# Five of eleven gate/up blocks of both SwiGLU sub-layers as seven products of halves, with the modulation sums at other blocks

## The chip, the cores and the metric

One core of a Trainium2 chip runs the whole layer in one launch. The metric is the device time of that core in microseconds, the median of three runs. Products run on TensorE (PE; its weight loads are PEld), elementwise work on VectorE (DVE), ScalarE (ACT) and GpSimd (POOL); SyncE (SP) issues the loads.

## What is computed

A decoder layer for 512 tokens of width 1024, all in float32. Only the two SwiGLU sub-layers and the conditioning bear on the change:

```python
def swiglu(h, w_gu, w_dn):
    g, u = jnp.split(h @ w_gu, 2, axis=-1)          # w_gu: 1024 x 5632, w_dn: 2816 x 1024
    return (jax.nn.silu(g) * u) @ w_dn

mods = (jax.nn.silu(c) @ w_ada[l] + b_ada[l]).reshape(B, N_MOD, 1, D_MODEL)
sh1, sc1, gt1, sh2, sc2, gt2, sh3, sc3, gt3 = [mods[:, i] for i in range(N_MOD)]
h = rmsnorm(x, g_pre[l, 0]) * (1 + sc1) + sh1
x = x + 0.5 * gt1 * rmsnorm(swiglu(h, w_gu1[l], w_dn1[l]), g_post[l, 0])
...
h = rmsnorm(x, g_pre[l, 2]) * (1 + sc3) + sh3
x = x + 0.5 * gt3 * rmsnorm(swiglu(h, w_gu2[l], w_dn2[l]), g_post[l, 2])
```

Between them stands the token mixer (gated linear attention beside softmax attention), which the change does not touch.

## The kernel before

**Products in three parts.** Every float32 operand is held as a pair of TensorE's float32r tiles, a rounded high part and the low part that is left (`hilo`, L197; for weights `split`, L152: ScalarE casts the raw tile to the high part at L155, VectorE subtracts at L156). A product is three matmuls, high by high, high by low and low by high (`PARTS`, L188).

**A gate/up block** (`ffn`, L381) makes 256 columns of gate and the same 256 of up, for 512 tokens; there are 11 blocks (jb = 0 to 10) in each of the two sub-layers. A block loads four raw weight tiles of 128 x 4 x 256 (512 KB each: `gw` and `uw`, first and second half of the 1024 input features), splits each, and issues 4 x 8 x 3 = 96 matmuls of 512 columns (`gu_matmuls`, L371) into four accumulators. Block 0 of the second sub-layer issues 192 of 256 columns instead, since its two halves of tokens come ready one after the other. The end of a block is tanh on ScalarE (L399), two fused operations on VectorE (L400, L401) and a high and a low part of the result (L403), twice.

**What sets the order.** A tile framework gives each tile a buffer from a ring by its tag and each engine a queue that it works through in order. The rings that matter: 4 raw tiles (`raw`, L148), 5 high and 5 low weight tiles (`whi`, `wlo`), 4 temporaries (`t2`), 69 units of 128 x 512, 6 accumulators (`mm`). A tile waits until the last reader of the tile that had its buffer is done. SyncE's queue holds the loads in the order of the program.

**The modulation sums** (`mod_cols`, L251) are columns of the conditioning for the next sub-layer: 8 loads of 256 KB into 4 raw tiles and 8 operations on VectorE (`ada_acc`, L202), then 4 tiny matmuls and 3 tiny operations. Four of them, handed over as `extra`, are taken in blocks 1, 3, 5 and 7 of the first sub-layer (L390). The second sub-layer has none.

`make_h` (L342) and `modulated` (L472) make the normalised input h of the second and the first sub-layer in temporaries and keep only its high and low parts.

Of the kernel before, what the change touches and what calls it, by code (L numbers as in the profile page):

```python
# [39 lines left out]
def tile_hybrid_layer(  # L40
# [24 lines left out]
    def tmp(shape=(P, 512), dt=F32):  # L65
        return sb.tile(list(shape), dt, tag="t2", bufs=NTMP, name=nm("t2"))
# [4 lines left out]
    def acc(shape=(P, 512)):  # L71
        return pm.tile(list(shape), F32, tag="mm", name=nm("mm"))
# [206 lines left out]
    def mod_gate(g, i, h, factor):  # L279

        c0 = (3 * i + 2) * D + h * 512
        gs = unit()
        g.append(gs)
        tc.keep_in_program_order(nc.sync.dma_start(gs, g_post[i, h * 512:(h + 1) * 512].partition_broadcast(P)))
        br = tmp()
        nc.sync.dma_start(br[0:1], b_ada[c0:c0 + 512].unsqueeze(0))

        def src(raw, kh):
            nc.sync.dma_start(raw, w_ada[kh * 256:(kh + 1) * 256, c0:c0 + 512].rearrange("(k p) c -> p k c", p=P))
        a = ada_acc(src)  # L290
        nc.vector.tensor_tensor(a[0:1, :], a[0:1, :], br[0:1], ALU.add)
        ps = aux()
        hi, lo = two_parts(a)
        nc.tensor.matmul(ps, ones_r, hi, start=True, stop=False)
        nc.tensor.matmul(ps, ones_r, lo, start=False, stop=True)
        nc.vector.scalar_tensor_tensor(gs, ps, factor, gs, ALU.mult, ALU.mult)
# [42 lines left out]
                nc.tensor.transpose(ps[:, j, e * P:(e + 1) * P], xn[e][d // 4][:, (d % 4) * P:(d % 4 + 1) * P], ident)  # L339
        return ps  # L340

    def make_h(tp, hs, shc, scc):  # L342

        xn = [x_norm(2 * tp + e, x_stat(2 * tp + e)) for e in range(2)]
        ts = slice(tp * 256, (tp + 1) * 256)
        for dp in range(4):
            ps = x_turned(tp, xn, dp)
            ht = tmp((P, 2, 256))
            for j in range(2):
                d = 2 * dp + j  # L350
                nc.vector.tensor_scalar(ht[:, j], ps[:, j], scc[:, d:d + 1], shc[:, d:d + 1], ALU.mult, ALU.add)
                hilo(hs[d][0][:, ts], hs[d][1][:, ts], ht[:, j], nc.gpsimd)
# [91 lines left out]
    with in_order(last):  # L444
        ada = []
        for ch in range(4):
            ada.append(ada_fetch_first(ch))
            if ch % 2 == 0:
                for b in first:
                    b.fetch(2 * ch, 2 * ch + 4)  # L450
        rs_ = []
        xn = []

        def norm(t):

            xx = sb.tile([P, D], F32, tag="wlo", bufs=NW, name=nm("xn"))
            for h in range(2):
                nc.vector.tensor_scalar(xx[:, h * 512:(h + 1) * 512], xt[t][h], rs_[t], None, ALU.mult)
            xn.append([xx[:, 0:512], xx[:, 512:1024]])

        for t in range(NT):
            rs_.append(x_stat(t))
            if t == 1:
                norm(0)
                small_columns()

        def turn(tp, dp, eng):
            ps = x_turned(tp, xn[2 * tp:2 * tp + 2], dp, (aux, acc)[dp % 2])
            for j in range(2):
                eng(xT[2 * dp + j][:, tp * 256:(tp + 1) * 256], ps[:, j])  # L470

        def modulated(ch, a, n):  # L472

            mod_turn(sh1, sc1, 0, ch, mod_reduce(a))
            ht = [tmp() for _ in range(2)]
            for e in range(2):
                d = 2 * ch + e
                nc.vector.tensor_scalar(ht[e], xT[d], sc1[:, d:d + 1], sh1[:, d:d + 1], ALU.mult, ALU.add)
            if ch < 3:
                ada_sum_a(ada[ch + 1], range(n))  # L480
            for e in range(2):
                d = 2 * ch + e
                hilo(hs[d][0], hs[d][1], ht[e])
            if ch < 3:
                ada_sum_a(ada[ch + 1], range(n, ROWS_A[ch + 1]))

        norm(1)
        norm(2)
        for dp in range(4):
            turn(0, dp, nc.vector.tensor_copy)  # L490
            if dp == 0:
# [649 lines left out]
```

## Time and profile before

| | us |
|---|---|
| median of 3 runs | 1454.02 (1453.26 to 1456.02) |
| profiled execution, its own time | 1452.96 |
| its span, first to last instruction | 1451.2 |
| TensorE busy | 1399.9 |
| VectorE busy | 765.7 |
| ScalarE busy | 531.4 |

The last three rows are busy time within the span. What lies around the span is 1452.96 - 1451.2 = 1.8 us. Matmuls are pipelined, so a duration of one matmul in the profile is longer than its share of the engine; start-to-start distances tell the rate. Durations on VectorE and ScalarE are those of one instruction; two that follow each other overlap by about 0.1 us.

### The profile page before, as it was taken

The numbers are of one execution on the slowest core, as the hardware profiler recorded it, in microseconds if no ns is written. First come the engines' busy times: TensorE is split into PE (matmuls) and PEld (weight loads), VectorE is DVE, ScalarE is ACT, GpSimd is POOL, SyncE is SP. The second block draws the span as 40 slices with busy tenths as digits, with TensorE's granted clock in tenths as the row PEclk, the third lists the DMA queues.
The fourth block names the chain that finished last, engine by engine and source line by source line (L and its number), as shares of the span: only waits on it lengthen the run. The fifth ranks groups of instructions, "written<-read, shape, count | busy, mean of one in ns | idle before, by whom it ended". The sixth has DMA issues, their size and how long they took to land.

```text
span 1451.2 us, 17081 instructions
## 1 busy us (share of the span) xinstructions
PE 1399.9 (96%) x6477; PEld 1124.3 (77%) x6477; DVE 765.7 (53%) x1210; ACT 531.4 (37%) x915; POOL 203.8 (14%) x328
## 2 busy tenths in 40 slices
PE   4899999999999999999999999999999999999998
PEld 3688888878877777767888887788888888887886
DVE  6945544372266689762745546538464334337232
ACT  5332322232244376653723333423353322222221
POOL 6200000000041643340110202100060000000001
PEclk7999999999999999999999999999999999999999
DMA  9444543272235846212232232125613223325411
GB/s 323 156 147 145 156 148 102 59 246 99 90 120 163 241 135 182 82 40 91 87 106 84 59 87 59 59 73 163 204 55 116 87 91 100 100 87 184 136 58 58
DMA packets 156463, 173.36 MB, mean 119 GB/s; under 512 B 8778, under 2 KB 123574, under 8 KB 156380
## 3 DMA queue, kind: packets, MB, share of 16 engines
q1 hardware_dynamic: 156380, 172.26, 38.4%
q8 instruction: 51, 0.84, 0.2%
q14 instruction: 32, 0.26, 0.1%
HBM read 168.00 MB, written 4.23 MB: 119 GB/s over the span
## 4 chain that ended last, share of the span: by engine, by line
PE 56%; DVE 4%; ACT 2%; issue 1%; POOL 1%; DMA 0%; DVEq 0%; POOLq 0%; ACTq 0%
PE mm L192 34%; PE mm L378 16%; PE aux L964 1%; PE aux L778 1%; PE mm L789 1%; DVE wlo L156 1%; ACT u L762 1%; PE mm L749 0%; PE mm L750 0%; DVE t L213 0%; DVE u L766 0%; POOL sm L310 0%; DVE u L753 0%; DMA raw<-in_w_dn_dram 0%; ACT jk L314 0%
## 5 line engine op out<-in xcount | busy, mean ns | idle before, releaser
L156 DVE TENSOR_TENSOR wlo<-raw,whi 128x1024 fp32r<-128x1024 f32 x218 | 271.9, 1250 | 405.1 <-ACT whi L155 397.1
L378 PE MATMUL mm<-u,whi 128*128 128x512 f32 (+1 forms) x1472 | 451.5, 390 | 10.3 <-ACT u L198 9.9
L155 ACT CAST whi<-raw 128x1024 fp32r<-128x1024 f32 x220 | 230.0, 1049 | 540.1 <-PE mm L192 294.8
L192 PE MATMUL mm<-whi,u 128*128 128x512 f32 x1216 | 390.1, 397 | 1.5 <-ACT u L198 1.5
L378 PEld LDWEIGHTS mm<-u,whi 128*128 128x128 f32 x1472 | 274.7, 190 | 75.5 <-ACT u L198 13.0
L192 PE MATMUL mm<-u,whi 128*128 128x512 f32 x896 | 288.2, 401 | 0.8 <-DVE u L991 0.8
L378 PE MATMUL mm<-u,wlo 128*128 128x512 f32 (+1 forms) x736 | 283.3, 389 | 0.0
L192 PEld LDWEIGHTS mm<-whi,u 128*128 128x128 f32 x1216 | 228.2, 188 | 54.2 <-ACT u L198 1.7
L192 PE MATMUL mm<-wlo,u 128*128 128x512 f32 x608 | 240.3, 395 | 0.0
L192 PEld LDWEIGHTS mm<-u,whi 128*128 128x128 f32 x896 | 166.2, 188 | 39.1 <-DVE u L991 1.2
L192 PE MATMUL mm<-u,wlo 128*128 128x512 f32 x448 | 177.9, 397 | 0.0
L378 PEld LDWEIGHTS mm<-u,wlo 128*128 128x128 f32 x736 | 139.5, 190 | 31.0
L192 PEld LDWEIGHTS mm<-wlo,u 128*128 128x128 f32 x608 | 114.2, 188 | 28.0
L192 PEld LDWEIGHTS mm<-u,wlo 128*128 128x128 f32 x448 | 84.4, 188 | 19.7
L307 POOL TENSOR_SCALAR sm<-ss 128x1 f32<-128x1 f32 x12 | 2.3, 190 | 667.1 <-ACT jk L314 667.1
L198 ACT CAST u<-t 128x512 fp32r<-128x512 f32 (+1 forms) x84 | 44.5, 537 | 113.9 <-DVE t L401 78.4
L213 DVE SCALAR_TENSOR_TENSOR t<-raw,csil,t 128x512 f32<-128x512 f32 x98 | 74.6, 762 | 2.7 <-DMA raw<-in_w_ada_dram 0.6
L737 POOL TENSOR_SCALAR u<-t,Ft 128x128 f32<-128x128 f32 (+1 forms) x64 | 41.7, 661 | 95.5 <-DMA t<-Fd 89.2
L400 DVE SCALAR_TENSOR_TENSOR t<-t,mm 128x512 f32<-128x512 f32 x44 | 30.1, 683 | 47.0 <-ACT t L399 47.0
L399 ACT ACTIVATE t<-mm 128x512 f32<-128x512 f32 x44 | 26.1, 594 | 63.3 <-PE mm L378 63.2
L401 DVE SCALAR_TENSOR_TENSOR t<-t,mm 128x512 f32<-128x512 f32 x44 | 30.2, 686 | 31.1 <-PE mm L378 29.4
L199 DVE TENSOR_TENSOR u<-t,u 128x512 fp32r<-128x512 f32 x52 | 35.6, 689 | 16.1 <-ACT u L198 15.9
(176 smaller groups left out, 1123.4 us busy)
## 6 DMA issues: line engine op xcount, KB each, us to landing
raw<-in_w_gu_dram SPq DMA_DIRECT2D x88, 512.0 KB, 3.6
raw<-in_w_in_dram SPq DMA_DIRECT2D x64, 512.0 KB, 3.8
raw<-in_w_dn_dram SPq DMA_DIRECT2D x44, 512.0 KB, 3.5
raw<-in_w_ada_dram SPq DMA_DIRECT2D x64, 256.0 KB, 3.1
raw<-in_w_ada_dram SPq DMA_DIRECT2D x24, 512.0 KB, 3.8
u<-in_w_ada_dram SPq DMA_DIRECT2D x32, 256.0 KB, 6.6
raw<-in_w_in_dram SPq DMA_DIRECT2D x16, 256.0 KB, 3.9
t<-Fd SPq DMA_DIRECT2D x16, 256.0 KB, 4.7
```

The source lines that it names most:

```text
L155: nc.scalar.copy(hi, raw)
L156: (eng or nc.vector).tensor_tensor(lo, raw, hi.bitcast(F32), ALU.subtract)
L192: nc.tensor.matmul(ps, a[i], b[j], start=first and n == 0, stop=last and n == 2)
L198: nc.scalar.copy(hi, src)
L199: (eng or nc.vector).tensor_tensor(lo, src, hi.bitcast(F32), ALU.subtract)
L213: nc.vector.scalar_tensor_tensor(a, raw[:, j, :], csil[:, k:k + 1], a, ALU.mult, ALU.add)
L378: nc.tensor.matmul(p_[:, ts], w_[k][i][:, cs], hs[k][e][:, ts], start=ks[0] == 0 and n == 0, stop=ks[-1] == KD - 1 and n == 3 * len(ks) - 1)
L399: nc.scalar.activation(th, pg, AF.Tanh, scale=0.5)
L400: nc.vector.scalar_tensor_tensor(th, th, 1.0, pg, ALU.add, ALU.mult)
L401: nc.vector.scalar_tensor_tensor(th, th, 0.5, pu, ALU.mult, ALU.mult)
L737: nc.gpsimd.tensor_scalar(s_at(s, i), fb[:, 0:n], -1.0, Ft[:, i, h:h + 1], ALU.mult, ALU.add)
L762: nc.scalar.activation(s_at(S[e], i), s_at(S[e], i), AF.Exp, bias=nmx[e][:, i:i + 1], accum_out=rs[e][:, i:i + 1])
```

## The change

Blocks 2, 3, 5, 6 and 7 of both sub-layers are made by `seven`. It takes the four raw tiles as a 2 x 2 matrix (a11, a12: gate by the first and second half of the features; a21, a22: up) and h as another (b11, b12, b21, b22: halves of the features by halves of the tokens), and forms the four quarters of the result from seven products of halves, with four sums of raw tiles on the left, four of quarters of h on the right (`right_sides`, made once, during block 1) and five sums of products. A product is 4 x 2 x 3 = 24 matmuls of 256 columns. For the right sides h is now kept in float32 too. The modulation sums go to the last four of the blocks that are left (`rest`: 4, 8, 9, 10).

```diff
+SEVEN = (2, 3, 5, 6, 7)
...
-    def make_h(tp, hs, shc, scc):
+    def make_h(tp, hs, shc, scc, keep=None):
...
-            ht = tmp((P, 2, 256))
+            ht = (tmp if keep is None else lambda s: unit(F32, s))((P, 2, 256))
+            if keep is not None:
+                keep[tp, dp] = ht
...
+    def right_sides(h4):
+        n, at = h4
+        sums = [[], [], [], []]
+        for k in range(0, 4, n):
+            b11, b12, b21, b22 = at(0, k), at(1, k), at(0, 4 + k), at(1, 4 + k)
+            t3, t1, t2, t4 = b12, unit(F32, (P, n, 256)), b22, b21
+            nc.vector.tensor_tensor(t1, b12, b11, ALU.subtract)
+            nc.vector.tensor_tensor(t3, b22, b12, ALU.subtract)
+            nc.vector.tensor_tensor(t2, b22, t1, ALU.subtract)
+            nc.vector.tensor_tensor(t4, b21, t2, ALU.subtract)
+            for to, t in zip(sums, (t1, t2, t3, t4)):
+                if k % 2 == 0:
+                    to.append((unit(F32R, (P, 2, 256)), unit(F32R, (P, 2, 256))))
+                hilo(*[part[:, k % 2:k % 2 + n] for part in to[-1]], t)
+        return [lambda k, e, s=s: s[k // 2][e][:, k % 2] for s in sums]
+
+    def seven(w_gu, jb, hs, rs, act):
+        gw, uw = gu_blocks(w_gu, jb)
+        for b in (gw, uw):
+            b.fetch()
+        a11, a12, a21, a22 = gw.raw[0], gw.raw[4], uw.raw[0], uw.raw[4]
+        t1, t2, t3, t4 = rs
+        b11, b21, b22 = [lambda k, e, k0=k0, ts=ts: hs[k0 + k][e][:, ts] for k0, ts in
+                         ((0, slice(0, 256)), (4, slice(0, 256)), (4, slice(256, 512)))]
+        sh = (4, 256)
+        l11 = split(a11, sh)
+        nc.vector.tensor_tensor(a21, a21, a22, ALU.add)
+        l1 = split(a21, sh)
+        nc.vector.tensor_tensor(a21, a21, a11, ALU.subtract)
+        l2 = split(a21, sh)
+        l22 = split(a22, sh)
+        nc.vector.tensor_tensor(a22, a22, a21, ALU.subtract)
+        l3 = split(a22, sh)
+        l12 = split(a12, sh)
+        nc.vector.tensor_tensor(a12, a12, a21, ALU.subtract)
+        l4 = split(a12, sh)
+        x, y, z = [acc((P, 2, 256)) for _ in range(3)]
+
+        def product(ps, left, right, first=False):
+            for k in range(4):
+                for j in range(2):
+                    for n, (i, e) in enumerate(PARTS):
+                        nc.tensor.matmul(ps[:, j], left[i][:, k, j * P:(j + 1) * P], right(k, e),
+                                         start=first and k + j + n == 0, stop=k == 3 and n == 2,
+                                         skip_group_check=True)
...
+        product(x, l11, b11, True)
+        p1 = tmp((P, 2, 256))
+        nc.scalar.copy(p1, x)
+        product(y, l2, t2, True)
+        u2 = plus(y, p1)
+        product(z, l1, t1, True)
+        product(y, l3, t3)
+        u3 = plus(y, p1)
+        up2 = plus(z, u3, u3)
+        product(x, l12, b21)
+        product(y, l22, t4)
+        product(z, l4, b22)
+        up1 = plus(y, p1, p1)
+        gate2 = plus(z, u2, u2)
+        a = [(unit(F32R), unit(F32R)) for _ in range(2)]
+        for h, (g, u) in enumerate(((x, up1), (gate2, up2))):
+            th = tmp((P, 2, 256))
+            nc.scalar.activation(th, g, AF.Tanh, scale=0.5)
+            nc.vector.scalar_tensor_tensor(th, th, 1.0, g, ALU.add, ALU.mult)
+            nc.vector.scalar_tensor_tensor(th, th, 0.5, u, ALU.mult, ALU.mult)
+            for j in range(2):
+                ts = slice(h * 256, (h + 1) * 256)
+                hilo(a[j][0][:, ts], a[j][1][:, ts], th[:, j])
+        act.extend(a)
...
+        rest = [b for b in range(KF // 2) if b not in by_seven][-len(extra):] if extra else []
...
+            if by_seven and jb == 1:
+                rs = right_sides(keep)
+            if jb in by_seven:
+                seven(w_gu, jb, hs, rs, act)
+                continue
...
-                late = extra.pop(0)() if extra and jb % 2 == 1 else None
+                late = extra.pop(0)() if jb in rest else None
```

`plus(ps, a)` is one VectorE sum of an accumulator and a tile. In the first sub-layer h is kept in `xT`, in its own place; in the second `make_h` keeps it in units. The lines of the changed kernel are one higher than those of the kernel before up to L340 (its L157 is L156 here, its L200 is L199), and its L488 and L489 are L400 and L401 here.

**VectorE between blocks 5 and 6 of the first sub-layer, before:** the end of block 5 (L400, L401, L199, tiny L275 to L277), with low parts of block 6's weights (`wlo_285`, `wlo_298`) between.

```order
L400 SCALAR_TENSOR_TENSOR t2_268_1347<-t2_268_1347,mm_263_1239 128x512
L401 SCALAR_TENSOR_TENSOR t2_268_1347<-t2_268_1347,mm_264_1240 128x512
L199 TENSOR_TENSOR u_270_1352<-t2_268_1347,u_269_1351 128x512
L156 TENSOR_TENSOR wlo_285_1384<-raw_283_1381,whi_284_1383 128x1024
L400 SCALAR_TENSOR_TENSOR t2_271_1355<-t2_271_1355,mm_265_1241 128x512
L401 SCALAR_TENSOR_TENSOR t2_271_1355<-t2_271_1355,mm_266_1242 128x512
L275 SCALAR_TENSOR_TENSOR scc_139_559<-aux_267_1339,cols_97 128x2
L276 TENSOR_TENSOR shc_138_558<-aux_267_1339,cols_97 128x2
L277 TENSOR_TENSOR scc_139_559<-scc_139_559,cols_97 128x2
L156 TENSOR_TENSOR wlo_298_1506<-raw_296_1503,whi_297_1505 128x1024
L199 TENSOR_TENSOR u_273_1360<-t2_271_1355,u_272_1359 128x512
L156 TENSOR_TENSOR wlo_301_1512<-raw_299_1509,whi_300_1511 128x1024
```

**The same place now**, from the last low part of block 5 (l4, `wlo_285`) to the third left side of block 6 (l2, `wlo_307`). L435 is `plus`: u3, up2, up1, gate2 in this order; L413 and L415 are the first two sums of raw tiles; `raw_300` and `raw_301` are a21 and a22 of block 6.

```order
L157 TENSOR_TENSOR wlo_285_1462<-raw_269_1427,whi_284_1461 128x1024
L157 TENSOR_TENSOR wlo_303_1674<-raw_298_1665,whi_302_1673 128x1024
L435 TENSOR_TENSOR t2_291_1568<-mm_287_1466,t2_289_1492 128x512
L435 TENSOR_TENSOR t2_291_1568<-mm_288_1467,t2_291_1568 128x512
L413 TENSOR_TENSOR raw_300_1669<-raw_300_1669,raw_301_1671 128x1024
L456 SCALAR_TENSOR_TENSOR t2_296_1649<-t2_296_1649,mm_286_1465 128x512
L157 TENSOR_TENSOR wlo_305_1679<-raw_300_1669,whi_304_1678 128x1024
L435 TENSOR_TENSOR t2_289_1492<-mm_287_1466,t2_289_1492 128x512
L415 TENSOR_TENSOR raw_300_1669<-raw_300_1669,raw_298_1665 128x1024
L457 SCALAR_TENSOR_TENSOR t2_296_1649<-t2_296_1649,t2_289_1492 128x512
L435 TENSOR_TENSOR t2_290_1518<-mm_288_1467,t2_290_1518 128x512
L157 TENSOR_TENSOR wlo_307_1684<-raw_300_1669,whi_306_1683 128x1024
```

Each left side of block 6 now stands behind sums that wait for products of block 5, and behind L413, which waits for two loads of block 6.

**VectorE at the start of block 1 of the first sub-layer, before:** the modulation sum (L213), then low parts of weights and the block's own end.

```order
L199 TENSOR_TENSOR u_145_573<-t2_143_568,u_144_572 128x512
L213 SCALAR_TENSOR_TENSOR t2_158_600<-raw_160_606,csil_98,t2_158_600 128x512 x2
L213 SCALAR_TENSOR_TENSOR t2_158_600<-raw_161_611,csil_98,t2_158_600 128x512 x2
L213 SCALAR_TENSOR_TENSOR t2_158_600<-raw_162_616,csil_98,t2_158_600 128x512 x2
L156 TENSOR_TENSOR wlo_176_748<-raw_174_745,whi_175_747 128x1024
L156 TENSOR_TENSOR wlo_179_754<-raw_177_751,whi_178_753 128x1024
L156 TENSOR_TENSOR wlo_182_760<-raw_180_757,whi_181_759 128x1024
L400 SCALAR_TENSOR_TENSOR t2_168_729<-t2_168_729,mm_163_621 128x512
L401 SCALAR_TENSOR_TENSOR t2_168_729<-t2_168_729,mm_164_622 128x512
L199 TENSOR_TENSOR u_170_734<-t2_168_729,u_169_733 128x512
```

**The same place now:** the right sides (L392 to L395 with their low parts at L200) between the first left sides of block 2.

```order
L392 TENSOR_TENSOR u_138_568<-u_28_117 128x256
L413 TENSOR_TENSOR raw_182_780<-raw_182_780,raw_183_782 128x1024
L393 TENSOR_TENSOR u_28_117<-u_32_121,u_28_117 128x256
L200 TENSOR_TENSOR u_140_574<-u_138_568,u_139_573 128x256
L394 TENSOR_TENSOR u_32_121<-u_32_121,u_138_568 128x256
L395 TENSOR_TENSOR u_32_121<-u_32_121 128x256
L200 TENSOR_TENSOR u_142_578<-u_32_121,u_141_577 128x256
L157 TENSOR_TENSOR wlo_187_790<-raw_182_780,whi_186_789 128x1024
L200 TENSOR_TENSOR u_144_582<-u_28_117,u_143_581 128x256
L415 TENSOR_TENSOR raw_182_780<-raw_182_780,raw_180_776 128x1024
L200 TENSOR_TENSOR u_146_586<-u_32_121,u_145_585 128x256
L392 TENSOR_TENSOR u_147_589<-u_29_118 128x256
```

The modulation sum has left the place; 32 instructions of 256 columns for the right sides stand there, of which these are the first.

## Rows read from the trace of the kernel before

**Rows 1.** The page's first part: span, and busy time (share of it) and instructions of each engine.

```profile
span 1451.2 us, 17081 instructions
...
PE 1399.9 (96%) x6477; PEld 1124.3 (77%) x6477; DVE 765.7 (53%) x1210; ACT 531.4 (37%) x915; POOL 203.8 (14%) x328
```

**Rows 2.** The page's slices: TensorE's granted clock in 40 equal slices, in tenths.

```profile
PEclk7999999999999999999999999999999999999999
```

**Rows 3.** The page's chain that ended last, by line.

```profile
PE mm L192 34%; PE mm L378 16%; PE aux L964 1%; PE aux L778 1%; PE mm L789 1%; DVE wlo L156 1%; ACT u L762 1%; PE mm L749 0%; PE mm L750 0%; DVE t L213 0%; DVE u L766 0%; POOL sm L310 0%; DVE u L753 0%; DMA raw<-in_w_dn_dram 0%; ACT jk L314 0%
```

**Rows 4.** Windows of one ordinary block of each sub-layer: columns in its first line.

```profile
core 0: us, PE busy (x) PEld busy (x) DVE busy (x) ACT busy (x) POOL busy (x), PEclk, DMA share, GB/s
109.95:132.45 22.50, 22.50 (x97) 18.08 (x96) 13.77 (x18) 6.54 (x8) 0.00 (x0) 1.00 0.60 187
1140.00:1162.50 22.50, 22.50 (x97) 18.08 (x96) 8.87 (x11) 6.44 (x9) 0.00 (x0) 1.00 0.30 93
```

**Rows 5.** Timeline of TensorE, 512 wide and 256 wide: start, us, instruction.

```profile
66.45 0.63 PE L378 MATMUL mm<-u,whi 128*128 128x512 f32 x2
...
86.84 0.63 PE L378 MATMUL mm<-u,whi 128*128 128x512 f32 x2
...
1082.13 0.40 PE L378 MATMUL mm<-u,whi 128*128 128x256 f32 x2
...
1092.34 0.40 PE L378 MATMUL mm<-u,whi 128*128 128x256 f32 x2
```

**Rows 6.** Groups by line and form: busy us, mean ns | idle before, and its releaser.

```profile
L156 DVE TENSOR_TENSOR wlo<-raw,whi 128x1024 fp32r<-128x1024 f32 x218 | 271.9, 1250 | 405.1 <-ACT whi L155 397.1 <-PE mm L192 6.1 <-PE aux L999 1.6
...
L155 ACT CAST whi<-raw 128x1024 fp32r<-128x1024 f32 x220 | 230.0, 1049 | 540.1 <-PE mm L192 294.8 <-issue 99.7 <-PE mm L378 80.8
...
L401 DVE SCALAR_TENSOR_TENSOR t<-t,mm 128x512 f32<-128x512 f32 x44 | 30.2, 686 | 31.1 <-PE mm L378 29.4
...
L199 DVE TENSOR_TENSOR u<-mm,u 128x512 fp32r<-128x512 f32 x20 | 13.5, 682 | 7.1 <-ACT u L198 7.1
...
L198 ACT CAST u<-t 128x256 fp32r<-128x256 f32 x32 | 12.6, 405 | 13.0 <-DVE t L351 12.2
...
L916 DVE TENSOR_TENSOR u<-u,u 128x256 f32<-128x256 f32 x28 | 11.6, 416 | 0.0
```

**Rows 7.** Timeline of ScalarE, then VectorE, in an ordinary block of the first sub-layer.

```profile
208.15 1.05 ACT L155 CAST whi<-raw 128x1024 fp32r<-128x1024 f32 x1 [3.48 <-DMA raw<-in_w_gu_dram]
...
209.23 1.23 DVE L156 TENSOR_TENSOR wlo<-raw,whi 128x1024 fp32r<-128x1024 f32 x1 [0.81 <-ACT whi L155]
210.37 0.74 DVE L213 SCALAR_TENSOR_TENSOR t<-raw,csil,t 128x512 f32<-128x512 f32 x1
...
224.56 0.68 DVE L400 SCALAR_TENSOR_TENSOR t<-t,mm 128x512 f32<-128x512 f32 x1
225.35 0.69 DVE L401 SCALAR_TENSOR_TENSOR t<-t,mm 128x512 f32<-128x512 f32 x1
```

**Rows 8.** SyncE's weight loads: issue in ns, us to landing; then five loads in a row.

```profile
L149 SPq DMA_DIRECT2D raw<-in_w_gu_dram x11: 367/368/368, 206.1 to 248.1; - x11
...
DMA to landing us min/median/max: 3.4/3.9/6.5
...
raw<-in_w_dn_dram SPq DMA_DIRECT2D x5, 512.0 KB, 5.4
```

**Rows 9.** Windows around pauses of TensorE: columns as in rows 4.

```profile
37.50:39.66 2.16, 0.09 (x1) 0.00 (x0) 1.93 (x3) 0.67 (x2) 1.18 (x1) 1.00 1.10 357
39.66:45.00 5.34, 5.31 (x15) 4.02 (x16) 5.27 (x5) 4.83 (x7) 2.90 (x2) 0.68 0.43 151
49.50:51.40 1.90, 0.03 (x1) 0.03 (x1) 1.63 (x4) 0.70 (x2) 0.56 (x1) 1.00 0.64 177
51.40:56.00 4.60, 4.58 (x18) 3.27 (x18) 4.40 (x7) 0.44 (x1) 0.00 (x0) 1.00 0.12 41
634.00:642.00 8.00, 6.83 (x30) 6.13 (x29) 5.06 (x20) 1.64 (x4) 1.45 (x3) 0.57 0.00 0
```

More of the change, by code (lines that the diff above doesn't have):

```diff
@@ L379, in gu_matmuls @@
                                  start=ks[0] == 0 and n == 0, stop=ks[-1] == KD - 1 and n == 3 * len(ks) - 1)
-    def ffn(w_gu, w_dn, hs, extra, gate, after, ps=None):
+    def right_sides(h4):
[13 more added lines that the diff above has]
+        return [lambda k, e, s=s: s[k // 2][e][:, k % 2] for s in sums]
@@ new lines, in seven, with plus @@
+    def seven(w_gu, jb, hs, rs, act):
[26 more added lines that the diff above has]
+                                         skip_group_check=True)
+        def plus(ps, a, out=None):
+            o = tmp((P, 2, 256)) if out is None else out
+            nc.vector.tensor_tensor(o, ps, a, ALU.add)
+            return o
+        product(x, l11, b11, True)
[22 more added lines that the diff above has]
+        act.extend(a)
@@ L383, in ffn @@
+    def ffn(w_gu, w_dn, hs, extra, gate, after, ps=None, by_seven=(), keep=None):
         act = []
+        rest = [b for b in range(KF // 2) if b not in by_seven][-len(extra):] if extra else []
         for jb in range(KF // 2):
+            if by_seven and jb == 1:
[3 more added lines that the diff above has]
+                continue
             if ps is None:
@@ L474, in modulated @@
             mod_turn(sh1, sc1, 0, ch, mod_reduce(a))
-            ht = [tmp() for _ in range(2)]
+            ht = xT[2 * ch:2 * ch + 2]
             for e in range(2):
@@ L522, in tile_hybrid_layer @@
     with not_before(last):
-        ffn(w_gu1[0], w_dn1[0], hs, extra, lambda g, h: mod_gate(g, 0, h, 0.5), after1, ps0)
+        ffn(w_gu1[0], w_dn1[0], hs, extra, lambda g, h: mod_gate(g, 0, h, 0.5), after1, ps0, SEVEN,
+            (1, lambda tp, k: xT[k][:, tp * 256:(tp + 1) * 256].unsqueeze(1)))
     hs = nxt[-1]
@@ L1097, in tile_hybrid_layer @@
     load_x(xd, True)
+    h3 = {}
     def after2(t):
@@ L1102, in after2 @@
         if t % 2:
-            make_h(t // 2, nxt[-1], sh3, sc3)
+            make_h(t // 2, nxt[-1], sh3, sc3, h3)
     down(w_out, mrg, lambda g, h: mod_gate(g, 1, h, 1.0), after2)
@@ L1110, in after3 @@
             nc.sync.dma_start(out[t * P:(t + 1) * P, h * 512:(h + 1) * 512], xt[t][h])
-    ffn(w_gu2[0], w_dn2[0], nxt[-1], [], lambda g, h: mod_gate(g, 2, h, 0.5), after3)
+    ffn(w_gu2[0], w_dn2[0], nxt[-1], [], lambda g, h: mod_gate(g, 2, h, 0.5), after3,
+        by_seven=SEVEN, keep=(2, lambda tp, k: h3[tp, k // 2]))
 _INS = ['x', 'c', 'w_ada', 'b_ada', 'g_pre', 'g_post', 'w_gu1', 'w_dn1', 'w_gu2', 'w_dn2',
```

## The prediction

> **What bounds the kernel now.** I read the page first. TensorE is busy for 1399.9 of 1451.2 us, VectorE for 765.7 [rows 1], and the chain that ended last runs for 50% of the span through the two matmul lines L192 and L378 [rows 3]; TensorE has its full clock nearly throughout [rows 2]. The windows then show what the stages differ in: an ordinary gate/up block lasts 22.50 us, TensorE is busy in all of it, VectorE for 8.87 us, or 13.77 us with a modulation sum [rows 4]. So in the gate/up stages TensorE sets the end, and VectorE has 9 to 14 us per block to spare. The change trades the first for the second.
>
> **The matmuls.** From 66.45 to 86.84 us lie 29 groups of three matmuls 512 wide: 20.39 / 87 = 0.2344 us each. From 1082.13 to 1092.34 us lie 29 groups 256 wide, with the kinds of operands and PSUM halves that the change uses: 10.21 / 87 = 0.1174 us, half [rows 5]. An ordinary block costs 96 x 0.2344 = 22.50 us, a product of the new kind 24 x 0.1174 = 2.82 us, a block of seven 19.72 us. Ten blocks save 10 x 2.78 = **27.8 us** if TensorE never waits. The Trainium skill's page "TensorE: Matmul & The Clock Gate", section "Back-to-back issue gap", speaks against this: it has a real stream's spacing set by the weight load too, 131 ns at 512 columns and 81 ns at 128. A straight line between them, my estimate, gives 98 ns at 256, by which a block would go from 12.6 to 16.4 us and the ten would lose 39 us. The rows at both widths decide against that here, so it gets no chance.
>
> **VectorE's work in a block of seven.** Seven low parts, as the L156 form, 1.14 us from start to start [rows 6, 7]. Four sums of raw tiles, a form that the trace lacks: 1024 columns from two float32 operands like L156, so between its spacing of 1.14 and twice the 512-wide 0.68 [rows 6]; I take 1.14, the same width. Five sums with an accumulator at 0.68, four operations like L401 at 0.69, four low parts 256 wide at 0.42 [rows 6]. Together 11 x 1.14 + 5 x 0.68 + 4 x 0.69 + 4 x 0.42 = **20.4 us against TensorE's 19.7**. ScalarE needs 7 x 1.05 + 3 x 0.6 + 4 x 0.41 = 10.8 us and is no bound. So VectorE has nothing left to spare in these blocks, and each wait at the head of its queue counts.
>
> **The waits.** I lay block 5's end of the first sub-layer out by hand with these prices, in the recorded order, t = 0 at its first product; products end at 2.82, 5.64, ... 19.74. The left sides come as l11, l1, l2, l22, l3, l12, l4 and rings of five buffers hold them. l4 gets l1's buffer after product 3 (8.46): cast, low part done at 11.0. Only then is the raw buffer of a12 free, and SyncE's queue holds block 6's a12 ahead of its a21 and a22, 0.37 us apart [rows 8]. Loads of 512 KB land 3.4 to 6.5 us after issue, five issued close together 5.4 [rows 8]; three at once stand nearest to the five, so a22 lands at 11.1 + 0.74 + 5.5 = 17.4. VectorE, done with up2 at 13.4, stands at L413 until then. Behind it in the queue: L413 to 18.5, L456 19.3, low part of l1 20.8, up1 21.4, L415 22.5, L457 23.3, gate2 23.9, low part of l2 **25.1**. TensorE ends block 5 at 19.74 and block 6's product 1 at 22.56, then waits 2.5 us.
>
> From there block 6 runs late: l3 holds product 4 for another 0.7 us, l4 is done at 36.7, a22 of block 7 lands at 43.1, and behind L413 the second half's operations of block 6 are queued too (8.8 us instead of 7.7), so l2 of block 7 is done at 51.9; product 1 ended at 45.5, product 3's first 13 matmuls fill part of the gap, and product 2 and l3 cost 4.7 + 1.0. Block 7 ends at 68.1 instead of 3 x 19.72 = 59.2: waits of 8.9 us. Then ordinary blocks follow, whose four low parts VectorE has in time.
>
> The same layout elsewhere: blocks 2 and 3 of the first sub-layer wait 4.4 us, since the 32 right-side instructions (32 x 0.42 = 13.4 us beside 9 us of block 1's own work in its 22.5 us) leave VectorE late for l4; in the second, 16 instructions 512 wide (10.9 us) leave it in time, 2.2 us. Blocks 5 to 7 of the second: L413 stands ahead of up2, so product 7 waits 2.0, product 4 of block 6 3.2, block 7 3.7: 8.9. Sum **24.4 us**. Handing over costs too: 0.03 us from the end of a cast to its low part [rows 7], 0.1 for a chained operation (0.79 between L400 and L401 against 0.68 [rows 7]); about 0.3 in each of six crossings, **2 us**.
>
> **The clock.** After TensorE stood still for 2.1 us at 37.5, the granted clock was 0.68 over the next 5.34 us, a loss of 5.34 x 0.32 = 1.7 us; after 1.9 us at 49.5 it stayed at 1.00 [rows 9]. 0.68 there is a mix of its two levels, 1.2 and 2.4 GHz. The layout has six pauses of 2.0 us or more. At each 1.7 us are lost, of which some 0.7 fall where the product would wait for VectorE anyway: 6 x 1.0 = **6 us**.
>
> **What moves at no cost.** The modulation sums, with their 8 loads each, leave blocks 1, 3, 5, 7 for 4, 8, 9, 10, all ordinary: 13.77 us of VectorE in 22.5 [rows 4] covers them there. On SyncE they now stand ahead of the weights of blocks 5, 9, 10 and of the first down tile; TensorE needs each a block later, 20 us against a landing of 6.5 at most [rows 8]. Without that cover one load would cost its landing, 3 to 7 us. Keeping h in float32 adds no instruction; units run short at block 7 (68 of 69 in use by my count at block 6), where t2's are free by then.
>
> **The sum** against the profiled execution: 1452.96 - 27.8 + 24.4 + 2 + 6 = 1457.6. The median of the runs stands 1.06 above that execution, so **1459 us**, 0.3% slower. A measurement of this kernel can tell 0.2% (2.9 us) from no change.
>
> **The rivals.**
> - *The loads land early.* If a22 lands 3.4 us after its own issue [rows 8], L413 starts at 15.2, l2 is done at 22.9, and the crossing from 5 to 6 costs 0.3. The three-block runs then wait 4.8 each, the pairs 2.0 and 0.5: 12 us; two pauses are left for the clock. 1454.0 - 27.8 + 12 + 2 + 2 = 1442, faster by 0.8%. It decides from a landing 3.8 us after a12's issue, which l2 needs for 22.56. For it: a single load's 3.4 to 3.9; against it: 1.5 MB in three loads.
> - *VectorE keeps up.* The queue's waits fall into TensorE's slack, and only 0.7 us of VectorE's surplus per crossing is left: 1454 - 27.8 + 4 = 1430. Against it: 20.4 us of work per block without a single wait.
> - *The clock falls for longer.* At 634 to 642 us the clock was 0.57, a loss of 3.4 us [rows 9]. If each of six pauses costs that, (1.7 more than taken), and raw sums take the upper price (0.22 us more each, two in each of six crossings), the sum grows by 10.2 + 2.6: 1472.
> - That the change does not do what it says can be left out: the order holds 168 matmuls of 256 columns in each of ten blocks.
>
> **Chances.** As summed 0.47, early loads 0.25, VectorE keeps up 0.13, the longer clock 0.15. The first case alone spans 1451 to 1468; it lies over 1456.9 with 0.33 and within 0.2% with 0.12. Early loads span 1438 to 1453: 0.20 faster, 0.05 the same. So faster 0.35, same 0.17, slower 0.48. Both signs hold much: 1459 is the likeliest, not a mean. The range 1440 to 1475 leaves out VectorE keeping up and a small part of the longer clock.
>
> **What would show it.** Right: 256-wide matmuls 0.117 us apart; VectorE busy by more than 85% from block 2 to 7, with its longest idle before L413 put to the load of raw tiles; TensorE idle before product 2 of blocks 3, 6 and 7, put to low parts of weights; granted clock under 1 behind these pauses; blocks 8 to 10 at 22.5 us. Wrong: TensorE without pauses over 1 us in blocks 2 to 7 (then 1430), or weight loads landing within 3.8 us (then 1442).

## The result and the profile after

The changed kernel takes **1438.1 us** (median of 4 runs, 1435.7 to 1438.7) against 1454.3 us before (1453.3 to 1456.0): ratio 0.9883, 95% interval 0.9868 to 0.9898. It is 1.2% faster, where I forecast 0.3% slower with a range of 1440 to 1475. The profiled execution took 1438.72 us, 14.2 less than that of before.

The page of the changed kernel, to be held against [rows 1] to [rows 3]: span and busy times, the granted clock in 40 slices, the chain by line.

```profile
span 1437.0 us, 18791 instructions
...
PE 1375.7 (96%) x7197; PEld 1141.2 (79%) x7197; DVE 894.2 (62%) x1398; ACT 577.2 (40%) x999; POOL 206.3 (14%) x328
...
PEclk9999999999999999999999999999999999999999
...
PE mm L193 34%; PE mm L381 8%; PE mm L429 3%; DVE wlo L157 2%; PE aux L1053 1%; ACT whi L156 1%; PE mm L878 1%; PE aux L867 1%; DMA raw<-in_w_gu_dram 1%; DVE t L214 1%; DVE u L855 1%; DVE u L200 0%; ACT u L851 0%; DVE u L842 0%; DMA raw<-in_w_dn_dram 0%
```

TensorE's busy time fell by 24.2 us and VectorE's rose by 128.5. The gate/up line (now L381) fell from 16% of the chain to 8%, the new product line L429 holds 3%, the low parts (L157, L156 before) rose from 1% to 2%, and the casts L156 and the load of gate/up weights came in with 1% each: in part of the span the chain now runs through VectorE and a load.

Windows of the changed kernel, columns in the first line: block 2 of the first sub-layer up to its last products, then the stretches that hold the blocks of seven.

```profile
core 0: us, PE busy (x) PEld busy (x) DVE busy (x) ACT busy (x) POOL busy (x), PEclk, DMA share, GB/s
89.59:109.30 19.71, 19.71 (x168) 19.70 (x167) 17.35 (x23) 7.66 (x10) 0.00 (x0) 1.00 0.27 81
...
60.00:300.00 240.00, 236.61 (x1435) 208.82 (x1434) 195.68 (x276) 94.70 (x136) 0.00 (x0) 1.00 0.46 141
1050.00:1320.00 270.00, 265.05 (x1649) 235.34 (x1648) 194.20 (x251) 109.33 (x167) 21.61 (x36) 1.00 0.33 102
```

168 matmuls of 256 columns take 19.71 us where TensorE doesn't wait, as priced from [rows 5]. TensorE stands still for only 3.4 and 5.0 us in the two long stretches, and the clock is 1.00 in both. None of the predicted clock losses is there.

Now the crossing from block 5 to 6 that the prediction laid out, t = 0 at 154.08. VectorE's timeline in the changed kernel (the pair at 158.81 is the low parts of l3 and l12, the pair at 164.10 those of l4 and of block 6's l11):

```profile
158.81 2.36 DVE L157 TENSOR_TENSOR wlo<-raw,whi 128x1024 fp32r<-128x1024 f32 x2 [1.17 <-ACT whi L156]
...
161.69 1.22 DVE L421 TENSOR_TENSOR raw<-raw,raw 128x1024 f32<-128x1024 f32 x1
164.10 2.36 DVE L157 TENSOR_TENSOR wlo<-raw,whi 128x1024 fp32r<-128x1024 f32 x2 [1.20 <-ACT whi L156]
166.38 1.41 DVE L435 TENSOR_TENSOR t<-mm,t 128x512 f32<-128x512 f32 x2
168.89 1.22 DVE L413 TENSOR_TENSOR raw<-raw,raw 128x1024 f32<-128x1024 f32 x1 [1.10 <-DMA raw<-in_w_gu_dram]
...
172.43 0.68 DVE L435 TENSOR_TENSOR t<-mm,t 128x512 f32<-128x512 f32 x1
173.03 1.22 DVE L415 TENSOR_TENSOR raw<-raw,raw 128x1024 f32<-128x1024 f32 x1
...
175.42 1.23 DVE L157 TENSOR_TENSOR wlo<-raw,whi 128x1024 fp32r<-128x1024 f32 x1
```

SyncE's timeline there, the three loads of block 6 that follow a11's (a12, a21, a22):

```profile
160.07 0.37 SPq L150 DMA_DIRECT2D raw<-in_w_gu_dram  x1
...
162.93 0.37 SPq L150 DMA_DIRECT2D raw<-in_w_gu_dram  x1
...
165.35 0.37 SPq L150 DMA_DIRECT2D raw<-in_w_gu_dram  x1
```

TensorE's timeline: products 1 and 2 of block 6, then the end of block 7's product 1 and its product 2.

```profile
173.88 0.40 PE L429 MATMUL mm<-u,whi 128*128 128x256 f32 x2
...
176.70 0.40 PE L429 MATMUL mm<-u,whi 128*128 128x256 f32 x2
...
196.58 0.28 PE L429 MATMUL mm<-u,wlo 128*128 128x256 f32 x1
198.51 0.73 PE L429 MATMUL mm<-u,whi 128*128 128x256 f32 x4 [1.65 <-ACT whi L156]
```

The low part of l4 ends at 165.3 (t = 11.2; predicted 11.0). But by then two of the three loads have been issued. The first went out at the end of l3's low part (158.81 + 1.22 = 160.03), the last read of a22; the second at the end of L421 (162.91), the last read of a21. Only the third waited for l4's buffer; it went out alone, and L413 could start 3.5 us after its issue. L413 starts at t = 14.8 instead of 17.4; from there to the end of l2's low part pass 7.8 us (predicted 7.7), and product 2 follows product 1 without a pause, where I had 2.5 us. The longest pause of the ten blocks is the 1.65 us at 196.86.

From here on I use one measure: a block of seven from its first matmul to the first of the next block, less 19.72, summed over all such blocks. It holds TensorE's pauses, what a lower clock costs and smaller delays. In the changed kernel that is **8.9 us** for ten blocks; the prediction had 24.4 of waits, 2 of hand-overs and 6 of the clock, 32.4.

### The profile page after: what moved, and what is told of

The parts are those of the page before. It is cut to its first block, busy times and chain, and to the rows that moved or that the text cites. A ratio compares the mean times of both kernels' runs of the same rounds, so it can differ in the third digit from the quotient of the medians.

```text
span 1437.0 us, 18791 instructions
## 1 busy us (share of the span) xinstructions
PE 1375.7 (96%) x7197; PEld 1141.2 (79%) x7197; DVE 894.2 (62%) x1398; ACT 577.2 (40%) x999; POOL 206.3 (14%) x328
## 4 chain that ended last, share of the span: by engine, by line
PE 51%; DVE 8%; ACT 2%; issue 2%; POOL 1%; DMA 1%; DVEq 0%; POOLq 0%; ACTq 0%
PE mm L193 34%; PE mm L381 8%; PE mm L429 3%; DVE wlo L157 2%; PE aux L1053 1%; ACT whi L156 1%; PE mm L878 1%; PE aux L867 1%; DMA raw<-in_w_gu_dram 1%; DVE t L214 1%; DVE u L855 1%; DVE u L200 0%; ACT u L851 0%; DVE u L842 0%; DMA raw<-in_w_dn_dram 0%
## 5 line engine op out<-in xcount | busy, mean ns | idle before, releaser
L157 DVE TENSOR_TENSOR wlo<-raw,whi 128x1024 fp32r<-128x1024 f32 x248 | 307.4, 1247 | 292.8 <-ACT whi L156 284.2
L156 ACT CAST whi<-raw 128x1024 fp32r<-128x1024 f32 x250 | 259.4, 1050 | 486.5 <-PE mm L193 300.6
L381 PE MATMUL mm<-u,whi 128*128 128x512 f32 (+1 forms) x832 | 249.4, 385 | 11.1 <-ACT u L199 9.9
L429 PE MATMUL mm<-u,whi 128*128 128x256 f32 x1120 | 199.6, 281 | 2.6 <-ACT whi L156 2.3
L193 PEld LDWEIGHTS mm<-u,whi 128*128 128x128 f32 x896 | 166.3, 188 | 39.1 <-DVE u L1080 1.2
L381 PEld LDWEIGHTS mm<-u,whi 128*128 128x128 f32 x832 | 153.4, 190 | 46.8 <-ACT u L199 13.2
L429 PEld LDWEIGHTS mm<-u,whi 128*128 128x128 f32 x1120 | 171.4, 188 | 4.2 <-ACT whi L156 3.4
L429 PE MATMUL mm<-u,wlo 128*128 128x256 f32 x560 | 157.1, 282 | 2.0 <-DVE wlo L157 2.0
L381 PE MATMUL mm<-u,wlo 128*128 128x512 f32 (+1 forms) x416 | 156.1, 382 | 0.0
L429 PEld LDWEIGHTS mm<-u,wlo 128*128 128x128 f32 x560 | 105.1, 188 | 3.3 <-DVE wlo L157 3.0
L193 PEld LDWEIGHTS mm<-u,wlo 128*128 128x128 f32 x448 | 84.4, 188 | 19.6
L381 PEld LDWEIGHTS mm<-u,wlo 128*128 128x128 f32 x416 | 79.4, 191 | 16.3
L199 ACT CAST u<-t 128x256 fp32r<-128x256 f32 (+1 forms) x80 | 35.9, 468 | 74.6 <-DVE t L489 47.2
```

The source lines that it names most:

```text
L156: nc.scalar.copy(hi, raw)
L157: (eng or nc.vector).tensor_tensor(lo, raw, hi.bitcast(F32), ALU.subtract)
L193: nc.tensor.matmul(ps, a[i], b[j], start=first and n == 0, stop=last and n == 2)
L199: nc.scalar.copy(hi, src)
L429: nc.tensor.matmul(ps[:, j], left[i][:, k, j * P:(j + 1) * P], right(k, e), start=first and k + j + n == 0, stop=k == 3 and n == 2, skip_g ...
```

## The experiments

My theory after reading both traces: one step was wrong, the one on whose release the three loads wait, and the rest of the layout was sound. The rival: the layout was too pessimistic elsewhere too, in VectorE's work or in what is queued behind L413. All times are medians. A ratio is to the kernel before, run beside each group of runs (1453.8 to 1454.6 us).

| kernel | us | ratio, 95% interval | excess of its blocks of seven, us |
|---|---|---|---|
| changed kernel | 1438.1 | 0.9883, 0.9868 to 0.9898 | 8.9 (10 blocks) |
| raw buffers held until l4 | 1463.4 | 1.0059, 1.0045 to 1.0072 | 34.3 |
| 5 raw buffers | 1435.6 | 0.9871, 0.9856 to 0.9886 | 4.6 |
| only the move | 1455.6 | 1.0008, 0.9999 to 1.0017 | none |
| move and right sides | 1456.8 | 1.0016, 1.0006 to 1.0027 | none |
| a12 loaded last | 1434.9 | 0.9868, 0.9854 to 0.9881 | 4.4 |
| a12 last, l11 on GpSimd | 1444.6 | 0.9933, 0.9921 to 0.9945 | 15.3 |
| blocks 2, 4, 6 only | 1438.4 | 0.9895, 0.9880 to 0.9910 | 0.0 (6 blocks) |
| changed kernel again | 1438.6 | 0.9888, 0.9873 to 0.9903 | 9.0 |
| a12 last again | 1433.6 | 0.9854, 0.9838 to 0.9871 | 4.3 |
| and blocks 2 to 7 in the second | 1432.5 | 0.9844, 0.9829 to 0.9859 | 6.6 (11 blocks) |
| and in the first | 1437.0 | 0.9881, 0.9866 to 0.9895 | 9.0 (12 blocks) |

**Give the loads the pattern of the prediction.** An operation of one column reads a21, a22 and l4's low part, so that all three buffers come free when l4 is done.

```diff
         l4 = split(a12, sh)
+        nc.vector.scalar_tensor_tensor(small(1), a21[:, 0, 0:1], a22[:, 0, 0:1], l4[1][:, 0, 0:1].bitcast(F32),
+                                       ALU.add, ALU.add)
```

> The changed kernel with one tiny VectorE operation (one column) at the end of each block of seven that reads a21, a22 and the low part of l4, so that all three raw buffers come free together, only when l4 is done, as the prediction had it. Theory (the hand-over of raw buffers was the wrong step: two of the three loads are really issued 2.4 and 5.3 us ahead of the end of l4): with the head start gone, L413 starts 5.5 to 6.5 us after the low part of l4 instead of 3.5, each of the six crossings between blocks of seven loses 1.5 to 2.5 us, the time rises from 1438 to 1447 to 1453, and TensorE's pauses ahead of product 2 reach 3 to 5 us. Rival (the waits were overestimated elsewhere, in VectorE's work or in what stands behind L413): 1438 to 1441 with pauses as they are.

Measured: 1463.4 us, 25 more than the changed kernel and 10 above the upper end of what even the theory expected. SyncE's timeline in this run, between blocks 5 and 6:

```profile
169.41 0.37 SPq L150 DMA_DIRECT2D raw<-in_w_gu_dram  x1
...
170.14 0.92 SPq L150 DMA_DIRECT2D raw<-in_w_gu_dram  x2
```

VectorE's timeline, ahead of the first raw sum L413 of block 6, then between blocks 6 and 7 (the low part of l4, then L413 of block 7), and TensorE's there:

```profile
174.80 0.69 DVE L437 TENSOR_TENSOR t<-mm,t 128x512 f32<-128x512 f32 x1 [1.47 <-PE mm L431]
...
176.29 1.23 DVE L413 TENSOR_TENSOR raw<-raw,raw 128x1024 f32<-128x1024 f32 x1
...
193.99 1.21 DVE L157 TENSOR_TENSOR wlo<-raw,whi 128x1024 fp32r<-128x1024 f32 x1
...
202.54 1.23 DVE L413 TENSOR_TENSOR raw<-raw,raw 128x1024 f32<-128x1024 f32 x1 [0.16 <-DMA raw<-in_w_gu_dram]
```

```profile
209.17 1.22 PE L431 MATMUL mm<-u,whi 128*128 128x256 f32 x4 [4.67 <-ACT whi L156]
```

Between blocks 6 and 7 the three loads leave within 1.2 us, L413 starts 7.3 us after l4's low part (3.6 in the changed kernel), and TensorE stands 4.67 us before product 2 of block 7. The edit also changed VectorE's order: up1 (L437 here, at 174.80), which waits for TensorE, now stands ahead of L413. So this is not a test of the loads alone; but at five of the six crossings L413 still waited for a load last (0.16 to 1.27 us). Windows of this run, columns as above: such pauses, and what follows them.

```profile
115.27:120.00 4.73, 4.73 (x28) 4.73 (x29) 4.23 (x5) 1.94 (x4) 0.00 (x0) 0.66 0.39 113
182.80:187.50 4.70, 4.70 (x27) 4.70 (x28) 4.22 (x5) 1.91 (x4) 0.00 (x0) 0.64 0.34 110
204.50:209.17 4.67, 0.00 (x1) 0.01 (x1) 3.56 (x6) 2.60 (x6) 0.00 (x0) 0.79 0.01 1
209.17:214.40 5.23, 5.23 (x25) 5.11 (x25) 4.09 (x4) 2.50 (x3) 0.00 (x0) 0.53 0.34 99
1150.04:1155.50 5.46, 5.46 (x25) 5.46 (x26) 4.23 (x5) 2.67 (x5) 0.00 (x0) 0.50 0.29 95
1242.31:1248.00 5.69, 5.69 (x26) 5.58 (x27) 4.55 (x4) 2.89 (x3) 0.00 (x0) 0.50 0.28 91
```

After the five pauses of 2.3 to 5.8 us the granted clock is 0.50 to 0.66 over the next 5 us, a loss of (1 - clock) x length = 1.6 to 2.8 us at each; 0.50 is the lower of its two levels, 1.2 GHz, throughout, the rest a mix with 2.4 GHz. The blocks' excess is 34.3 us against the 32.4 that I had summed. The rival falls: with the loads about as I had assumed them, waits of the predicted size come back. That the sums agree so well is in part luck: the five pauses add up to 19.3 us (3.18, 2.33, 4.67, 3.30 and 5.78; I had 24.4 of waits and 2 of hand-overs), the clock behind them to 11.3 us in these windows (I had 6).

**Five raw buffers, and a12 loaded last.** Both free L413 from l4's buffer, the second without any memory: a12 is then the load that waits, and its first use is the sixth low part.

```diff
-NU = 69
-NRAW = 4
+NU = 67
+NRAW = 5
```

> The changed kernel with 5 raw buffers instead of 4, and 67 units instead of 69, which pays for them in SBUF. Theory (L413 waits for the third load, the one that waits for l4's buffer): the wait of L413 for its load, 1.1 to 1.2 us at its head, goes, and most of the 8 to 9 us that TensorE still waits in blocks 2 to 7 with it: 1431 to 1434. Rival (VectorE's own 20.4 us a block against 19.7 sets these waits): 1436 to 1439, with VectorE busy without a gap and TensorE's pauses as before.

```diff
-        for b in (gw, uw):
-            b.fetch()
+        gw.fetch(0, 4)
+        uw.fetch()
+        gw.fetch(4)
```

> The changed kernel with the four loads of a block of seven issued in the order a11, a21, a22, a12 instead of a11, a12, a21, a22; still 4 raw buffers. Theory (the third load of the three waits for l4's buffer, and L413 waits for that third load): now a12 is the one that waits, and nobody needs it before the sixth low part, so L413 no longer waits for a load: as with five raw buffers, 1434 to 1436.5. Rival (what five raw buffers brought was not L413's wait): 1437.5 to 1439.5, as the changed kernel.

Measured: 1435.6 and 1434.9 us. What VectorE waited before the first raw sum (us in total, times), in the changed kernel and then with a12 last, by their views of that line (now L414):

```profile
L413 DVE TENSOR_TENSOR raw<-raw,raw x10: 1219/1226/1226, 73.8 to 1211.3; 128x1024 f32<-128x1024 f32 x10
...
  DMA raw<-in_w_gu_dram: 12.4, 8
```

```profile
L414 DVE TENSOR_TENSOR raw<-raw,raw x10: 1214/1220/1228, 72.0 to 1204.7; 128x1024 f32<-128x1024 f32 x10
...
  DMA raw<-in_w_gu_dram: 3.8, 3
```

The waits fell from 12.4 us at 8 of 10 places to 3.8 at 3, and the excess from 8.9 to 4.4. Of the 12.4 only 5.7 stand between two blocks of seven, and of these 0.5 are left; the other places follow ordinary blocks, where VectorE has time. The theory's mechanism holds; five buffers brought 2.5 us, less than the 4 to 7 expected: about half of the excess is not put to a load, and stays. Beside each other on one chip:

> The changed kernel itself once more, beside the three runs that follow on the same chip, so that they can be compared with it directly: 1436 to 1439 by either theory.

> The kernel with a12 loaded last once more, on the same chip as the changed kernel. Theory (L413's wait for its load was worth what the first run showed): 2 to 4 us below the changed kernel. Rival (the first difference came from the chips): within 1 us of it.

1438.6 us (1437.8 to 1439.6) and 1433.6 us (1432.9 to 1434.1): 5.0 us from the order of four loads (2 to 4 expected).

**The parts that I had costed at nothing.** First the move of the modulation sums, with h kept in float32 as in the changed kernel, then the sums of the right sides too.

```diff
         rest = [b for b in range(KF // 2) if b not in by_seven][-len(extra):] if extra else []
+        by_seven = ()
```

```diff
-            if jb in by_seven:
+            if False:
```

> No block by seven products and no sums of right sides; the modulation sums still move to blocks 4, 8, 9 and 10, and h stays in float32. The prediction's theory (the move costs nothing): 1452.5 to 1456, as before the change. Rival (the move itself gives or takes something: four blocks without VectorE's extra 5 us, or SyncE's loads ahead of the down weights): a difference of 2 us or more, seen at the first blocks or at the down stage.

> As the run that moves only the modulation sums, but with the sums of the right sides made in block 1 of both sub-layers and never used; all blocks ordinary. The prediction's theory (block 1's 22.5 us of TensorE hide the 13.4 and 10.9 us of VectorE): within 1 us of that run. Rival (they delay the low parts of block 1's or block 2's weights): 2 to 5 us more, with a pause of TensorE in block 1 or 2.

Measured: +1.2 us, with an interval that holds zero, and +2.3 (0.9 to 3.9), which leaves the right sides between theory and rival. No pause appears in block 1 or 2. Together with the blocks this closes the account: 1454.3 - 27.8 + 8.9 + 2.3 = 1437.7 against 1438.1. The changed kernel's profile shows where a part of the 2.3 us lies: GpSimd's, VectorE's and TensorE's timelines in block 0 of the second sub-layer.

```profile
1068.85 1.70 POOL L200 TENSOR_TENSOR u<-u,u 128x256 fp32r<-128x256 f32 x1
...
1068.22 1.75 DVE L157 TENSOR_TENSOR wlo<-raw,whi 128x1024 fp32r<-128x1024 f32 x1
...
1070.61 0.39 PE L381 MATMUL mm<-u,whi 128*128 128x256 f32 x1 [1.01 <-POOL u L200]
```

TensorE waits 1.01 us for the last of GpSimd's low parts of h, which takes 1.70 us beside a VectorE operation instead of 0.73. All runs in which h is kept have this pause (0.96 to 1.03 us), the run with the move among them; before, TensorE waits there for GpSimd at most 0.18 us. In that run keeping h is the only change to the second sub-layer, and from there on its profile is 1.3 us longer than that of before. So keeping h, which adds no instruction, changed what runs beside what. What the move itself costs is therefore not shown, and the rest of the 2.3 us I did not locate.

**Blocks of seven without neighbours.** `SEVEN = (2, 4, 6)`.

> The changed kernel with blocks 2, 4 and 6 of both sub-layers by seven products, so that no two stand next to each other; the modulation sums go to blocks 7 to 10. Theory (a block of seven saves 2.78 us, and only neighbours wait for each other): six blocks save 16.7 us, less about 1: 1438 to 1440, per block 2.5 to 2.8. Rival (each block of seven has a cost of its own at its start or end, neighbours or not): 1442 to 1446, per block 1.5 to 2.

Measured: 1438.4 us, 15.4 below before, 2.6 a block, as the theory had it. Windows of two of these blocks, columns as above:

```profile
130.50:150.20 19.70, 19.70 (x169) 19.66 (x168) 15.93 (x19) 9.56 (x12) 0.00 (x0) 1.00 0.51 159
172.70:192.40 19.70, 19.70 (x169) 19.66 (x168) 15.92 (x19) 9.57 (x12) 0.00 (x0) 1.00 0.53 161
```

TensorE is busy from end to end, and the excess is 0.0: what is missing from 16.7 us lies outside these blocks. Six blocks set apart gain as much as the change's ten with neighbours.

**Relieve VectorE.** The low part of l11 goes to GpSimd, on top of a12 last.

```diff
-        l11 = split(a11, sh)
+        l11 = split(a11, sh, nc.gpsimd)
```

> As the run with a12 loaded last, and the low part of l11 made by GpSimd (2.6 us there, 1.2 on VectorE) in every block of seven. Theory (with the loads out of the way VectorE's 20.4 us against 19.7 sets the waits that are left): VectorE falls to 19.3 us a block, below TensorE, and the 4 to 6 us that blocks 2 to 7 still lose against 7 products of 2.82 us go: 1430 to 1432. Rival (the operations of the two engines get in each other's way, or the waits come from the chain cast, low part, sum alone): no gain, 1434 to 1438.

Measured: 1444.6 us, 9.7 more than with a12 last alone and worse than theory and rival had it. GpSimd's timeline, and VectorE's beside it, then the durations (min/median/max, ns) of that line in this run:

```profile
162.08 2.40 POOL L157 TENSOR_TENSOR wlo<-raw,whi 128x1024 fp32r<-128x1024 f32 x1 [22.26 <-ACT whi L156]
183.53 2.47 POOL L157 TENSOR_TENSOR wlo<-raw,whi 128x1024 fp32r<-128x1024 f32 x1 [19.05 <-ACT whi L156]
```

```profile
1157.11 0.68 DVE L436 TENSOR_TENSOR t<-mm,t 128x512 f32<-128x512 f32 x1
...
162.40 3.16 DVE L414 TENSOR_TENSOR raw<-raw,raw 128x1024 f32<-128x1024 f32 x1 [1.12 <-DMA raw<-in_w_gu_dram]
...
185.00 2.09 DVE L414 TENSOR_TENSOR raw<-raw,raw 128x1024 f32<-128x1024 f32 x1 [1.22 <-DMA raw<-in_w_gu_dram]
```

```profile
L414 DVE TENSOR_TENSOR raw<-raw,raw x10: 1210/2080/3219, 70.3 to 1210.7; 128x1024 f32<-128x1024 f32 x10
```

L414 takes 1.22 us alone. Here it ends at 165.56 and 187.09, that is 1.08 and 1.09 us after GpSimd's operation (164.48 and 186.00): it did not run slower, it stood until GpSimd was done. At all seven places where L414 starts within GpSimd's operation it ends 1.1 us after it, whether it takes 1.61 or 3.22 us. The sum L436, with one input in an accumulator and one in SBUF, takes its usual 0.68 us at 1157.11, beside GpSimd's operation of 1157.06 to 1159.46. The Trainium skill's page "SBUF — State Buffer", section "SBUF: two separate sides", has this: an operation of VectorE with two inputs in SBUF and one of GpSimd that reads SBUF hold their shared ports as an exclusive lock, for the whole instruction. The rows agree with a lock, not with shared bandwidth. So the 1.2 us taken from VectorE came back as up to 2.0 us, at the head of the chain that TensorE waits for. That is not all of the 9.7 us: L414 also waited 6.9 us for loads (3.8 without GpSimd), and the clock fell after two of TensorE's pauses. How much each brought is not shown. Windows of this run after a pause of 1.82 us, after which the clock fell, and after one of 2.06, after which it did not:

```profile
182.79:187.80 5.01, 5.01 (x29) 5.01 (x30) 3.43 (x3) 1.14 (x2) 2.47 (x1) 0.66 0.66 206
1208.62:1213.60 4.98, 4.98 (x42) 4.98 (x43) 3.84 (x4) 0.95 (x2) 2.51 (x1) 1.00 0.63 201
```

**Longer runs of neighbours**, on top of a12 last: block 4 by seven in the second sub-layer, then in the first too, with two modulation sums in block 10.

```diff
-        by_seven=SEVEN, keep=(2, lambda tp, k: h3[tp, k // 2]))
+        by_seven=(2, 3, 4, 5, 6, 7), keep=(2, lambda tp, k: h3[tp, k // 2]))
```

```diff
-SEVEN = (2, 3, 5, 6, 7)
+SEVEN = (2, 3, 4, 5, 6, 7)
...
-        rest = [b for b in range(KF // 2) if b not in by_seven][-len(extra):] if extra else []
+        rest = (8, 9, 10, 10) if extra else ()
...
-                late = extra.pop(0)() if jb in rest else None
+                late = [extra.pop(0)() for b in rest if b == jb]
...
-                if late:
-                    late()
+                for f in late:
+                    f()
```

> As the kernel with a12 loaded last, and in the second sub-layer block 4 also by seven products, so that blocks 2 to 7 are six neighbours. Theory (VectorE's 20.4 us against TensorE's 19.7 cost a neighbour 0.7 us, whatever the length of the run): 2.78 saved, 0.7 to 1.4 given back, 1.4 to 2.1 us below the kernel with a12 last. Rival (the ordinary block 4 was where VectorE caught up; without it lateness piles up): no gain, or up to 4 us more.

> As the run before, and block 4 of the first sub-layer by seven products too; its modulation sum moves to block 10, which then makes two (8.87 + 2 x 4.9 = 18.7 us of VectorE by the windows of before, in 22.5). Theory as for that run: another 1.4 to 2.1 us less. Rival (lateness piles up, or two sums with 16 loads in block 10 are too much ahead of the first down tile): no gain, or up to 5 us more.

Measured: 1432.5 us (1430.8 to 1433.2), 1.1 below a12 last, too little to be told from it (1.4 to 2.1 expected); and 1437.0, where its rival had up to 5 us more. The last run's windows over two neighbours in the middle of its six, and over the start of the down stage; then TensorE's timeline there:

```profile
149.90:170.50 20.60, 20.33 (x170) 19.86 (x169) 19.69 (x25) 10.09 (x14) 0.00 (x0) 1.00 0.35 103
170.50:191.10 20.60, 20.34 (x170) 19.86 (x169) 19.69 (x25) 10.09 (x14) 0.00 (x0) 1.00 0.33 103
...
290.00:295.00 5.00, 3.90 (x8) 2.68 (x9) 3.56 (x4) 2.38 (x3) 0.00 (x0) 0.58 0.98 329
295.00:300.00 5.00, 5.00 (x18) 3.94 (x17) 4.10 (x7) 0.00 (x0) 0.00 (x0) 0.74 0.82 241
```

```profile
290.87 1.65 PE L193 MATMUL mm<-whi,u 128*128 128x512 f32 x3 [2.13 <-ACT whi L156]
```

Lateness doesn't pile up: neighbours settle at 20.6 us each, VectorE busy for 19.69 of them, so each gives back 0.9 us of its 2.78. What the last run lost stands elsewhere: the loads of the second modulation sum went ahead of down weights, TensorE stood 2.13 us, and the clock was 0.58 and 0.74 over the next 10 us (2.1 + 1.3 us). The cover that I had named for moved loads ends there.

## Why the prediction was wrong

- **The matmuls** were right: 2.82 us a product, 19.71 us a block; the six blocks without neighbours have no excess.
- **VectorE's work** was 1 us too high: 20.4 us forecast, 19.69 us busy a block where neighbours follow each other long enough. Only the 1024-wide forms were priced from start to start; a sum with an accumulator was put at its duration of 0.68, but the next operation starts 0.60 us after it (172.43 to 173.03). At such distances (1.14, 0.60, 0.60 and 0.34) the sum is 19.3. That a block settles at 20.6 all the same is in part luck: VectorE is idle for 0.9 us of it, more than I had for handing over.
- **The waits: the step that failed** is "Only then is the raw buffer of a12 free, and SyncE's queue holds block 6's a12 ahead of its a21 and a22 ... so a22 lands at 17.4". I had given each load of block 6 the buffer of its namesake in block 5. By the times of issue the buffers go to the next loads in the order in which they come free: a12 takes a22's, a21 takes a21's after L421, and only a22 takes the buffer that l4 frees. That put L413 2.6 us earlier, and the 24.4 us of waits fell to about 9. The time that I gave three loads issued together, 5.5 us from the last one's issue, was not too long: in the run with held buffers it was up to 6.2. The order of the VectorE and SyncE instructions, which I had, gives the last reader of each buffer; I did not work out who inherits it.
- **The clock** was a consequence: with no pause over 1.65 us, none of the 6 us arose. Its size per pause was underestimated: 1.7 us (1.0 beyond what VectorE would hold up anyway), where the run with held buffers shows 1.6 to 2.8.
- **What moves at no cost** cost about 2 us together with the right sides, a term that I had put at nothing. "Keeping h in float32 adds no instruction" is true, but it brought a pause of 1.0 us.
- **The rival "the loads land early"** gave 1442 and was the nearest. Its condition, a22 landing 3.4 us after its own issue, was met (3.5), and L413 started at 14.8 where it had 15.2. But the reason was not one it gave: it let all three loads wait for l4's buffer and leave 0.37 us apart, while a22 left alone, 5.3 us after a12. By its other measure, 3.8 us from a12's issue to a22's landing, it would have failed: 8.8 us lie between them. So that it came near is in part luck.
- **The rival "VectorE keeps up"** (1430) came near only once a12 was loaded last, at 1433.6.
- The range's lower end was set too high for the chances given: 1440 cut off the lower end of the early loads' own span, 1438 to 1453, and the measured time lies there.

## What to carry to other kernels

When a pool's buffers limit prefetching, write down for each buffer its last reader and which load inherits it; one load in three waiting for the late buffer is a different kernel from three. Then order the loads so that the one that waits is the one used last: that was worth 5.0 us here, a third of what the change itself brought, for three lines. Before moving elementwise work from VectorE to GpSimd, look at which VectorE operations with two SBUF inputs would run beside it.

## What the runs showed of the hardware

- VectorE's 1024-column sum of two SBUF tiles, 1.22 us alone, took up to 3.2 us beside a GpSimd operation of 2.4, and ended 1.1 us after it. A low part of 256 columns on GpSimd, 0.73 us alone, took 1.70 beside a low part of VectorE.
- TensorE's clock read 0.50 to 0.66 over some 5 us after pauses of 2.3 to 5.8 us. Among shorter ones the length alone does not tell: after 1.65 us in the changed kernel it stayed at 1.00 (the row below), after 1.82 us in the run with GpSimd it read 0.66, after 2.06 us in the same run 1.00.

```profile
198.51:203.50 4.99, 4.99 (x42) 4.99 (x43) 4.92 (x7) 2.27 (x5) 0.00 (x0) 1.00 0.34 104
```

- In the run with held buffers a22, the last of three loads issued within 1.2 us, let L413 start 6.2 us after its own issue (196.38 to 202.54); alone, in the changed kernel, 3.5.
